# An RMSNorm kernel: two pairs of queued transfers each joined into one

## The chip, the cores and the metric

The kernel runs on one core of a Trainium2 chip. A core has separate engines with their own instruction streams: TensorE (PE in the profile), VectorE (DVE), ScalarE (ACT), GpSimd (POOL) and SyncE (SP), which here only issues transfers. Transfers between the chip's main memory (HBM) and the on-chip memory (SBUF, 128 partitions) are carried out by sixteen DMA engines that all transfers share. The metric is the time of one execution on the device in microseconds. Several executions are timed; one further execution is recorded by the profiler.

## The reference

Every row of 512 values is divided by the root of its mean square and multiplied by gamma:

```python
def setup_inputs():
    batch, seq, dim = 16, 1024, 512
    return {
        "x": np.random.randn(batch, seq, dim).astype(np.float32),
        "gamma": np.ones(dim, dtype=np.float32),
    }

def reference(x, gamma):
    eps = 1e-5
    rms = np.sqrt(np.mean(x ** 2, axis=-1, keepdims=True) + eps)
    return (x / rms * gamma).astype(np.float32)
```

The input is 16,384 rows, 33.55 MB, and the output has the same size.

## The kernel before

The 16,384 rows are cut into four tiles t = 0 to 3 of 128 partitions times 32 rows (`R = 32`); one partition holds 32 rows that lie one after another in HBM, 64 KB. A tile is thus 8.39 MB, and "rows a to b" of a tile means rows a to b - 1 of every partition, so 16 rows are 4.19 MB. Three tiles fit in SBUF: `slots[0..2]`. Tile 3 is loaded into slot 0, so it can be loaded only when tile 0 has been stored from there. Results are written over the data in the slot and stored from there.

Work goes in nine groups (`groups`, L76): tile 0 in rows 0:7, 7:16 and 16:32, every other tile in two halves 0:16 and 16:32. For each group:

- ScalarE squares the rows in pieces of 7, 5, 4 (or 9) rows, and VectorE sums the squares of each row (`square_sums`, L96 and L97). The squares lie in PSUM (`sq_psum`) or SBUF (`sq_sbuf`).
- `inverse_rms`: ScalarE takes the root (L102) and VectorE the reciprocal (L103).
- The last rows of the group (`share`, mostly 7) are multiplied by GpSimd alone, by the row factor and then by gamma (`scale_by_pool`, L109 and L110). The other rows (mostly 9) are multiplied by the row factor on ScalarE, one instruction per row (`scale`, L118), and then by gamma on VectorE in one instruction for all of them (`times_gamma`, L122).

The order is written by hand (`tc.manual_schedule()`); each engine takes its instructions in program order. The loop (L163) handles the scaling of group k and, interleaved with it, the squares and sums of group k + 1: first GpSimd's scaling, then the first two pieces of squares of the next group, then half of ScalarE's row scalings, the third piece of squares, the rest of the row scalings, VectorE's multiplication by gamma, and last the transfers that this group makes possible (`transfers`, L129) and the next group's root and reciprocal. So on ScalarE, the squares of the first half of tile 3 stand ahead of the row scalings of the second half of tile 2.

Loads (`load`, L45) are all issued by SP. Stores (`store`, L49) are issued by SP too, but for three small ones of 4 rows that ScalarE issues: rows 0:4 and 4:8 of tile 0 and rows 0:4 of tile 1. A queue of transfers is worked off in the order of issue; an issue waits on the issuing engine until all that it depends on is done, and what stands behind it in that engine's program waits too. A store waits for VectorE and GpSimd to have finished its rows. A load of tile 3 waits for the completion of the stores that empty its part of slot 0. An instruction that reads loaded rows waits for the whole transfer that brings them.

SP's program is: rows 0:1 and 1:8 of tile 0, gamma in five pieces, rows 8:16 and 16:32 of tile 0, both halves of tile 1, rows 0:23 of tile 2; then, when the group (0, 16) is done, what L133 to L138 list; then the stores of tile 1 rows 4:32, of all of tile 2, and of both halves of tile 3. Rows 23:32 of slot 2 are loaded late because they serve as room for squares of 9 rows until then (L91).

Of the kernel before, what the change touches and what calls it, by code (L numbers as in the profile page):

```python
# [9 lines left out]
def kernel(  # L10
# [33 lines left out]
    def load(t, slot, r0, r1):  # L44
        dma = nc.sync.dma_start(out=slots[slot][:, r0:r1], in_=xv[t][:, r0:r1])  # L45
        before_scale.append((slot, r0, r1, dma))

    def store(t, slot, r0, r1, queue=nc.sync):
        dma = queue.dma_start(out=ov[t][:, r0:r1], in_=slots[slot][:, r0:r1])  # L49
        before_scale.append((slot, r0, r1, dma))  # L50
# [78 lines left out]
    def transfers(t, g):  # L129
        if (t, g) == (0, 0):  # L130
            load(1, 1, 16, 32)
            load(2, 2, 0, 23)
        elif (t, g) == (0, 16):  # L133
            store(0, 0, 8, 16)
            store(0, 0, 16, 32)
            load(2, 2, 23, 32)
            load(3, 0, 0, 16)
            load(3, 0, 16, 32)  # L138
        elif (t, g) == (1, 16):
            store(1, 1, 4, 32)  # L140
        elif (t, g) == (2, 16):
            store(2, 2, 0, 32)
        elif (t, g) == (3, 0):
            store(3, 0, 0, 16)
        elif (t, g) == (3, 16):
            store(3, 0, 16, 32)
# [16 lines left out]
    for k, group in enumerate(groups):  # L163
        t, g, n, pieces, share = group
        mine = n - share
        half = (mine + 1) // 2
        ahead = groups[k + 1 :][:1]
        ss, todo = pieces_of(ahead[0]) if ahead else (None, [])
        scale_by_pool(rstd, t, g, n, share)
        for piece in todo[:2]:  # L170
            square_sums(*piece)
        if (t, g) == (0, 7):
            store(0, 0, 0, 4, nc.scalar)
        scale(rstd, t, g, 0, half)
        for piece in todo[2:]:
            square_sums(*piece)
        scale(rstd, t, g, half, mine)
        if (t, g) == (0, 16):
            store(0, 0, 4, 8, nc.scalar)
        elif (t, g) == (2, 0):  # L180
            store(1, 1, 0, 4, nc.scalar)
        times_gamma(t, g, 0, mine)
        transfers(t, g)
        for nxt in ahead:
            rstd = inverse_rms(ss, nxt[2])
# [30 lines left out]
```

## Time and profile before

| | us |
|---|---|
| median of 3 runs | 161.56 (161.45 to 161.64) |
| the profiled execution | 161.69 |
| its span, first to last instruction | 159.8 |
| DVE busy in the span | 112.0 (70%) |
| ACT busy | 107.8 (67%) |
| POOL busy | 106.4 (67%) |
| moved by DMA in the span | 67.12 MB, mean 420 GB/s |

The span is what the trace covers; 1.9 us of the profiled execution lie around it. The profile divides the span into 40 slices and gives each engine's busy share as a digit; the DMA line is the mean share of the sixteen DMA engines. A DMA queue q1 carries what SP issues, q10 what ScalarE issues. "Us to landing" is the time from the issue of a transfer to its completion, so it contains the time spent behind earlier transfers. The trace also has a record of each DMA packet (one packet per partition and transfer of x or out here, so eight on each of the sixteen engines); where start and end of a transfer on the DMA engines are named, they are read from these records.

### The profile page before, as it was taken

The numbers are of one execution on the slowest core, as the hardware profiler recorded it, in microseconds if no ns is written. First come the engines' busy times: TensorE is split into PE (matmuls) and PEld (weight loads), VectorE is DVE, ScalarE is ACT, GpSimd is POOL, SyncE is SP. The second block draws the span as 40 slices with busy tenths as digits, with TensorE's granted clock in tenths as the row PEclk, the third lists the DMA queues.
The fourth block names the chain that finished last, engine by engine and source line by source line (L and its number), as shares of the span: only waits on it lengthen the run. The fifth ranks groups of instructions, "written<-read, shape, count | busy, mean of one in ns | idle before, by whom it ended". The sixth has DMA issues, their size and how long they took to land.

```text
span 159.8 us, 273 instructions
## 1 busy us (share of the span) xinstructions
PE 2.0 (1%) x2; PEld 0.5 (0%) x2; DVE 112.0 (70%) x39; ACT 107.8 (67%) x108; POOL 106.4 (67%) x24
## 2 busy tenths in 40 slices
PE   0050000000000000000000000000000000000000
PEld 0010000000000000000000000000000000000000
DVE  0019098899798999999999999999999009800000
ACT  3071966975999999999899999989970990000000
POOL 1000960994999599999999999999999990000000
DMA  5999999999999998998999999999996997999995
GB/s 179 431 427 468 443 418 410 377 449 408 455 476 443 443 410 365 423 500 370 434 468 394 470 445 390 501 459 459 459 476 279 525 476 312 394 468 451 394 435 222
DMA packets 2747, 67.12 MB, mean 420 GB/s; under 512 B 313, under 2 KB 314, under 8 KB 442
## 3 DMA queue, kind: packets, MB, share of 16 engines
q1 hardware_dynamic: 2314, 63.97, 93.5%
q10 hardware_dynamic: 432, 3.15, 4.7%
q14 instruction: 1, 0.01, 0.0%
HBM read 33.56 MB, written 33.55 MB: 420 GB/s over the span
## 4 chain that ended last, share of the span: by engine, by line
DVE 59%; ACT 21%; DMA 4%; issue 1%; ACTq 1%; SPq 0%
DVE ss L97 36%; DVE slot L122 23%; ACT slot L118 8%; ACT slot L96 8%; ACT sq_psum L96 5%; DMA slot<-in_x_dram 4%; DVE ss L103 1%; ACT ss L102 0%; ACTq L211 0%; ACT gamma_b L162 0%; SPq L45 0%; ACTq L49 0%; ACTq L96 0%
## 5 line engine op out<-in xcount | busy, mean ns | idle before, releaser
L109 POOL TENSOR_TENSOR slot<-slot,ss 128x3584 f32<-128x3584 f32 (+2 forms) x9 | 46.9, 5213 | 24.2 <-DVE ss L103 24.2
L110 POOL TENSOR_TENSOR slot<-slot,gamma_b 128x3584 f32<-128x3584 f32 (+2 forms) x9 | 59.2, 6582 | 0.7
L97 DVE TENSOR_REDUCE ss<-sq_psum 128x7 f32<-128x3584 f32 (+1 forms) x13 | 42.2, 3245 | 13.7 <-ACT sq_psum L96 13.7
L118 ACT ACTIVATE slot<-slot,ss 128x512 f32<-128x512 f32 x75 | 47.2, 706 | 4.7 <-DVE ss L103 4.7
L122 DVE TENSOR_TENSOR slot<-slot,gamma_psum 128x4608 f32<-128x4608 f32 (+2 forms) x9 | 41.3, 4589 | 8.7 <-ACT slot L118 8.7
L96 ACT ACTIVATE sq_psum<-slot 128x3584 f32<-128x3584 f32 (+1 forms) x13 | 34.5, 2657 | 6.3 <-DMA slot<-in_x_dram 5.7
L97 DVE TENSOR_REDUCE ss<-slot 128x9 f32<-128x4608 f32 x3 | 14.9, 4954 | 4.4 <-ACT slot L96 4.2
L97 DVE TENSOR_REDUCE ss<-sq_sbuf 128x5 f32<-128x2560 f32 x5 | 14.0, 2800 | 0.0
L96 ACT ACTIVATE slot<-slot 128x4608 f32<-128x4608 f32 x3 | 12.1, 4032 | 0.0
L96 ACT ACTIVATE sq_sbuf<-slot 128x2560 f32<-128x2560 f32 x5 | 11.6, 2324 | 0.3 <-DMA slot<-in_x_dram 0.3
L102 ACT ACTIVATE ss<-ss,eps_t 128x16 f32<-128x16 f32 (+2 forms) x9 | 2.7, 304 | 11.7 <-DVE ss L97 11.7
L103 DVE RECIPROCAL ss<-ss 128x16 f32<-128x16 f32 (+2 forms) x9 | 2.1, 235 | 0.4 <-ACT ss L102 0.4
L66 PE MATMUL gamma_psum<-gamma_row,ones_col 1*128 1x512 f32 x2 | 2.0, 1122 | 8.7 <-DMA gamma_row<-in_gamma_dram 8.7
L72 ACT ACT_TABLE_LOAD x1 | 1.3, 1283 | 1.2 <-PEq L200 1.2
L162 ACT COPY gamma_b<-gamma_psum 128x512 f32<-128x512 f32 x1 | 0.6, 564 | 0.0
L66 PEld LDWEIGHTS gamma_psum<-gamma_row,ones_col 1*128 1x128 f32 x2 | 0.5, 305 | 8.6 <-issue 8.6
L64 POOL MEMSET ones_col<- 1x128 f32 x1 | 0.2, 194 | 0.3 <-POOLq L200 0.3
L200 POOL MEMSET const-float32-0.0<- 128x1 f32 x1 | 0.1, 98 | 0.2 <-issue 0.2
L72 ACT ACTIVATE table<-eps_t 128x1 f32<-128x1 f32 x1 | 0.2, 202 | 0.0
L200 POOL MEMSET const-bfloat16-1.0<- 128x1 bf16 x1 | 0.1, 101 | 0.0
L200 POOL MEMSET const-uint8-127<- 128x1 uint8 x1 | 0.1, 101 | 0.0
L200 POOL MEMSET const-float32-1.0<- 128x1 f32 x1 | 0.1, 98 | 0.0
(1 smaller groups left out, 0.1 us busy)
## 6 DMA issues: line engine op xcount, KB each, us to landing
slot<-in_x_dram SPq DMA_DIRECT2D x5, 4096.0 KB, 25.0
out_dram<-slot SPq DMA_DIRECT2D x3, 4096.0 KB, 20.2
out_dram<-slot SPq DMA_DIRECT2D x1, 7168.0 KB
slot<-in_x_dram SPq DMA_DIRECT2D x1, 5888.0 KB
out_dram<-slot ACTq DMA_DIRECT2D x3, 1024.0 KB
slot<-in_x_dram SPq DMA_DIRECT2D x1, 2304.0 KB, 25.7
slot<-in_x_dram SPq DMA_DIRECT2D x1, 2048.0 KB, 10.0
out_dram<-slot SPq DMA_DIRECT2D x1, 2048.0 KB
```

Source lines behind the costliest of these rows:

```text
L66: nc.tensor.matmul(gamma_psum[:, 0], ones_col, gamma_row, start=True, stop=True)
L72: nc.scalar.activation(out=table, in_=eps_t, func=AF.Sqrt)
L96: nc.scalar.activation(out=sq[:, :m], in_=rows, func=AF.Square)
L97: nc.vector.tensor_reduce(out=ss[:, r : r + m, 0], in_=sq[:, :m], axis=mybir.AxisListType.X, op=OP.add)
L102: nc.scalar.activation(out=ss[:, :n, 0], in_=ss[:, :n, 0], func=AF.Sqrt, bias=eps_t, scale=1.0 / D)
L103: nc.vector.reciprocal(out=ss[:, :n, 0], in_=ss[:, :n, 0])
L109: nc.gpsimd.tensor_tensor(out=part, in0=part, in1=by_row, op=OP.mult)
L110: last = nc.gpsimd.tensor_tensor(out=part, in0=part, in1=gamma_b.to_broadcast([P, share, D]), op=OP.mult)
L118: nc.scalar.activation(out=x[:, g + r, :], in_=x[:, g + r, :], func=AF.Copy, scale=rstd[:, r])
L122: scaled = nc.vector.tensor_tensor(out=part, in0=part, in1=gamma_psum.to_broadcast([P, r1 - r0, D]), op=OP.mult)
L162: nc.scalar.copy(out=gamma_b[:, 0], in_=gamma_psum[:, 0])
L200: nc = _bacc.Bacc("TRN2", target_bir_lowering=False, num_devices=1)
```

## The change

When group (0, 16) is done, SP issued two stores of tile 0, rows 8:16 and 16:32, and after the rest of tile 2 two loads of tile 3, rows 0:16 and 16:32. Now it issues one store of rows 8:32 and one load of rows 0:32. Nothing else in the program is changed; the same bytes are moved.

```diff
         elif (t, g) == (0, 16):
-            store(0, 0, 8, 16)
-            store(0, 0, 16, 32)
+            store(0, 0, 8, 32)
             load(2, 2, 23, 32)
-            load(3, 0, 0, 16)
-            load(3, 0, 16, 32)
+            load(3, 0, 0, 32)
         elif (t, g) == (1, 16):
             store(1, 1, 4, 32)
```

SP issues 19 transfers instead of 21, gamma's five among them; the order of instructions on the other engines is as before. What waits for what follows the transfers: the store of rows 8:32 waits for both groups in it, the load of tile 3 for every store that empties slot 0, and every instruction that reads tile 3 for the whole load.

## The prediction

> **What bounds the kernel now.** I read the page first: the three compute engines are each busy about 70% of the span, the DMA line of part 2 stands at 9 almost from end to end, and part 3 puts the two hardware queues together at 98% of sixteen engines.
>
> ```profile
> span 159.8 us, 273 instructions
> DMA  5999999999999998998999999999996997999995
> q1 hardware_dynamic: 2314, 63.97, 93.5%
> q10 hardware_dynamic: 432, 3.15, 4.7%
> ```
>
> So the transfers set the end, whatever the chain of waits says (it ends in a DVE multiplication, because it cannot see behind a store that sits in a queue). Queue q1 is SP's, q10 ScalarE's. The question for any change is then whether the queue ever runs empty. Next I asked for SP's issues in order of time, and for DMA answers over short windows, which give the time from issue to landing of one transfer.
>
> SP's issues around the change; columns: start, length, engine, line (a merged row's length runs to the end of its last issue):
>
> ```profile
> 39.78 16.01 SPq L49 DMA_DIRECT2D out_dram<-slot  x2
> 55.83 0.43 SPq L45 DMA_DIRECT2D slot<-in_x_dram  x1
> 66.45 10.20 SPq L45 DMA_DIRECT2D slot<-in_x_dram  x2
> 111.67 0.34 SPq L49 DMA_DIRECT2D out_dram<-slot  x1
> 125.65 13.94 SPq L49 DMA_DIRECT2D out_dram<-slot  x2
> ```
>
> Store 8:16 of the first tile is issued at 39.78, store 16:32 at 55.45 (39.78 + 16.01 less one issue of 0.34), the rest of tile 2 at 55.83, the halves of tile 3 at 66.45 and 76.33, the store of tile 2 at 111.67, the last store at 139.25. From the short windows, the remainder of tile 2 and the first half of tile 3, with us to landing at the end:
>
> ```profile
> slot<-in_x_dram SPq DMA_DIRECT2D x1, 2304.0 KB, 25.7
> slot<-in_x_dram SPq DMA_DIRECT2D x1, 4096.0 KB, 25.1
> ```
>
> They land at 55.83 + 25.7 = 81.5 and 66.45 + 25.1 = 91.55. Twenty-five microseconds for 4 MB that need ten says that each lies behind other work. The pace of the queue comes from the window 80.6:90.3, which holds just the first half of tile 3 (4.19 MB in 9.7 us, nothing else moving):
>
> ```profile
> q1 hardware_dynamic: 144, 4.19, 100.2%
> ```
>
> That is 2.42 us per MB. Who uses that half is in the timeline (start, length, engine, line, operation):
>
> ```profile
> 91.61 0.31 ACT L102 ACTIVATE ss<-ss,eps_t 128x16 f32<-128x16 f32 x1 [0.35 <-DVE ss L97]
> 91.82 3.14 ACT L96 ACTIVATE sq_psum<-slot 128x3584 f32<-128x3584 f32 x1
> 96.52 3.82 DVE L97 TENSOR_REDUCE ss<-sq_psum 128x7 f32<-128x3584 f32 x1
> 105.18 4.94 DVE L122 TENSOR_TENSOR slot<-slot,gamma_psum 128x4608 f32<-128x4608 f32 x1
> ```
>
> The square at 91.82 reads rows 0:7 of tile 3 and starts 0.3 us after they land: no slack on this load. Behind that square, on the same in-order engine, stand the row scalings of tile 2's second half, and behind those DVE's multiplication (105.18 to 110.12) that its store waits for.
>
> **Part one, the merged store.** It removes one issue (0.34 us of SP) and holds back rows 8:16 (2.1 MB) from 39.78 to 55.45, when rows 16:32 are ready. Cover: the load of tile 2's first 23 rows still runs; by the packet records of the trace it ends at 60.6 to 61.1 (first engine to last), 5.2 us after the issue. An issue into an empty queue needs about 1.0 us to its first packet: the first load is issued at 0.74, and the window to 1.7 holds no packet, that to 1.8 two. So the queue does not run dry, the order of bytes stays, and the two stores together still end at 75.7. With the cover gone the price would be up to 1.0 us. Joining two transfers saves what a boundary costs: by the packet records the 6.3 MB take 14.54 us for twelve packets per engine of 1.21 us (14.5), so at most 0.05 us. Cost: 0.
>
> The Trainium skill, page "DMA: Bandwidth & Descriptors", section "Anatomy of one DMA", gives every transfer about 2.0 us of fixed cost beside its bytes; by it two transfers fewer would take 4 us off. The row above (100.2% of the engines busy while transfers queue behind one another) disagrees for queued transfers.
>
> **Part two, the merged load.** Three things move. (a) Its issue: it now waits for the merged store as a whole (76.26), so at 76.33, where the first half had gone out at 66.45. Cover: the remainder of tile 2 moves until 80.6 to 81.1, 4.3 us against 1.0 needed. Bounds: 0, or 0.3 if the 4.6 us that ScalarE's store of 27.41 took to its first packet (in a loaded queue) held here; I take 0, since SP's own transfers follow each other without a hole. (b) SP's following stores wait behind this issue, at 76.33 as before; the next is due at 83.68: 0. (c) The landing. Rows 0:16 no longer have a completion of their own: the square of 91.82 waits for all 8.4 MB. They start at 80.6 and need 8 x 2.42 = 19.35 us on each engine, so the last engine ends at 100.5, and completion takes 0.4 to 0.7 more: 100.9 to 101.2 undisturbed.
>
> ScalarE's store of tile 1's rows 0:4 (1.05 MB, 2.4 us) is issued at 86.70 and may fall inside. Its packets, windows 86:90.3 and 90.3:102.6:
>
> ```profile
> q1 hardware_dynamic: 48, 1.57, 84.7%
> q10 hardware_dynamic: 144, 1.05, 20.2%
> ```
>
> No q10 packet before 90.3; then all of it between the packets of the second half, one 8 KB packet to one of 32 KB. In all three such stores an engine starts three more SP packets after the issue before q10's first. Bounds: 0 and 2.4 us. With SP packets of 64 KB (2.42 us) three of them reach to about 95, which leaves two to alternate with, so two q10 packets of 0.31: 0.6 us. Landing: 101.7, ends 100.9 and 103.6.
>
> The Trainium skill (same page, section "Queues, rings and completion order") has an engine change between queues only after a packet of some 9 to 17 descriptors; by that this store would wait for the whole load and the landing be 101.0. The one-to-one alternation above speaks against it.
>
> **From the landing to the end.** The square starts 0.08 after landing (8.28 to 8.37 at the first load): 101.78, 9.96 late. The ScalarE chain behind it, taken from the iteration where ScalarE did not wait for DVE (81.61 on): square of 7 rows 3.08, of 5 rows 2.23, five scalings 3.06, square of 4 rows 1.80, four scalings 2.54, together 12.7. DVE's reductions keep up (the third ends at 12.5), so DVE's multiplication starts at 114.5 and ends at 119.45: 9.33 late; 0.6 is won back because DVE had been the later one here. SP issues tile 2's store at 119.5; before, 111.67.
>
> Where was the queue meanwhile? The last store is issued at 139.25 and lands 19.7 later, at 158.95; going back from its last packet (158.6) by 10.2, 9.7 and 19.35 us, tile 2's store had its first packets at 119.35. So it had waited 7.7 us in the queue, and the last store 9.1. After the change the queue is empty from 119.4 to 119.9 (the same bytes went before) and the store's first packet comes at 119.5 + 1.0 = 120.5: a hole of 0.6 to 1.1 us. From there DVE runs without a stop as before (110.12 to 139.19 is 29.07), while the DMA needs 29.0 for the two stores in between: the last store is issued at 148.6, first packet 149.6 instead of 148.35. POOL, 1.3 us ahead of DVE's needs before, restarts with the reciprocal at 119.7 and ends its rows of group (3,0) at 133.7; that store is due at 139.8. So 1.0 to 1.2 us later at the end; I take 1.1.
>
> Sum: 161.69 (the profiled execution; 1.9 of it lies around the span) + 1.1 = 162.8. The median of the runs is 0.13 below that execution: 162.7. As a formula: end moves by landing + first-packet delay - 101.46.
>
> **The rivals.** Full mixing: the ScalarE store falls wholly inside the load, as it did in the second half before. Landing 103.6: + 3.0 to 3.1, 164.6. For it: the row of 90.3:102.6. Against: that mixing began only 3.7 us after the issue, with packets half as long.
>
> Hidden after all (the not-slower side): place, the empty queue at 119.4; it decides at landing + delay = 101.46. If ScalarE's store stays out (100.9) and a store needs between its issue's own 0.34 us and 0.56 us to its first packet, nothing is lost: 161.6 (161.9 with the delay of 1.0). For it: the store had 7.7 us of waiting in the queue to give, against 9.3 of delay, so it is close. Against: 1.0 us in the only row with an empty queue, and the early joining of q10.
>
> The packet rule of the Trainium skill above points this way, and so does its HWDGE first-byte figure of about 0.6 us (same page, section "Latency and other measured facts"): with both the time would be 161.7. No run here shows that figure.
>
> Slow issue: the 3.7 to 4.6 us that ScalarE's stores needed to a first packet are the issue itself and not a wait behind fetched packets. At 119.5 that gives a hole of over 4: 3.7 to 4.6 in place of 1.0 is + 3.8 to 4.7, 165.4 to 166.3. Against: the first load's 1.0 us.
>
> Faster: boundaries between transfers cost more than the rows show, and two fewer pay while the stall stays hidden. By the rows the gain is 2 x 0.05 at most, 161.5; more needs a hole that no window shows. By the fixed cost of the Trainium skill's page "DMA: Bandwidth & Descriptors" it would be 4 us, 157.6.
>
> **How the numbers follow.** My forecast (161.9 to 163.6, landing about 101 to 102.4) 0.62; full mixing 0.14; hidden 0.11; slow issue 0.08; faster 0.05. A change within 0.2% (0.32 us) cannot be told from none here. The range leaves out faster and slow issue and reaches from the hidden case to full mixing: 161.5 to 164.7. Faster 0.05, within 0.11, slower 0.84.
>
> **What would show it.** Right: a single wait of ScalarE's square on the load, some 9 to 10 us long, ending near 101.8; POOL and DVE idle behind it; SP's issue of tile 2's store near 119.5 and a dip of the DMA line right there; none at 61 and 80. Wrong: a landing at 103 or later, a dip at 61 or 80, or a DMA line that stays full at 119 with the end unmoved.

## The result, and the profile after

The changed kernel takes 162.96 us (median of 5 runs, 162.92 to 163.33), the kernel before 161.56 us beside it (161.45 to 161.66). The ratio is 1.0089, with a 95% interval of 1.0076 to 1.0101: slower by 0.9%, 1.4 us. The profiled execution took 162.92 us with a span of 161.1.

The page of the changed kernel, part 1's head, the DMA line and the queues:

```profile
span 161.1 us, 270 instructions
DMA  5999999899999999998999696998979969999996
q1 hardware_dynamic: 2026, 63.97, 92.6%
q10 hardware_dynamic: 432, 3.15, 4.6%
```

The bytes are those of before, 63.97 and 3.15 MB; the sixteen engines need the same time for them, but it is a smaller share of a longer span. A slice is 4 us long and a packet of 64 KB is entered at its start, so the 6s and 7s between the 9s do not all mean idleness. The waits of the changed kernel say more (columns: engine and line, whom it waited for, us in total, times, longest):

```profile
POOL slot L109 <- DVE ss L103: 32.8, 5, 15.0
DVE ss L97 <- ACT sq_psum L96: 22.9, 5, 11.4
ACT sq_psum L96 <- DMA slot<-in_x_dram: 15.9, 2, 10.4
```

Before, ScalarE had one such wait on a load in this line, 5.7 us at the start:

```profile
ACT sq_psum L96 <- DMA slot<-in_x_dram: 5.7, 1, 5.7
```

Now there is a second of 10.4 us. The timeline shows which, and what stands behind it:

```profile
102.17 3.16 ACT L96 ACTIVATE sq_psum<-slot 128x3584 f32<-128x3584 f32 x1 [10.37 <-DMA slot<-in_x_dram]
105.37 3.89 DVE L97 TENSOR_REDUCE ss<-sq_psum 128x7 f32<-128x3584 f32 x1 [8.89 <-ACT sq_psum L96]
114.95 4.96 DVE L122 TENSOR_TENSOR slot<-slot,gamma_psum 128x4608 f32<-128x4608 f32 x1 [0.20 <-ACT slot L118]
```

The square of tile 3's first rows started at 91.82 and starts at 102.17; the multiplication of tile 2's second half started at 105.18 and starts at 114.95. From windows and the timeline, the issue of the load at 76.06 with its time to landing, the issue of tile 2's store, and the two last issues:

```profile
slot<-in_x_dram SPq DMA_DIRECT2D x1, 26.1
119.98 0.34 SPq L49 DMA_DIRECT2D out_dram<-slot  x1
134.19 15.22 SPq L49 DMA_DIRECT2D out_dram<-slot  x2
```

The load is complete at 102.15. The store of tile 2 was issued at 111.67 and is issued at 119.98, and the last one at 149.07 (134.19 + 15.22 - 0.34) in place of 139.25. What that does to the queue is seen in the window 117 to 122, forty slices of 0.125 us in which a packet is entered where it starts; first the kernel before, then the changed one:

```profile
DMA  0999999000000000009999990000000000000099
GB/s 0 918 1376 2294 1376 918 459 0 0 0 0 0 0 0 0 0 0 0 1049 1573 2622 2097 524 524 0 0 0 0 0 0 0 0 0 0 0 0 0 0 1573 2621
```

```profile
DMA  9999000000000000000000000000009900000000
GB/s 2753 1376 1376 1376 0 0 0 0 0 0 0 0 0 0 0 0 0 0 0 0 0 0 0 0 0 0 0 0 0 0 3670 4719 0 0 0 0 0 0 0 0
```

Before, the next round of packets starts some 2.1 us after the last round, which is as long as a packet of the store of tile 1 takes (2.12 us). After, 3.5 to 3.8 us pass. By the packet records the engines are idle for 1.55 us each on average between 116 and 124 (time of the window less the packets' time, over the sixteen engines), and for nothing measurable anywhere else where the change could have opened a hole (55 to 65, 76 to 86, 144 to 152). Before, none of the four windows had idle time. The hole is about as long as the loss of 1.4 us.

### The profile page after: what moved, and what is told of

Read it like the earlier page. It is cut to its first block, busy times and chain, and to the rows that moved or that the text cites. A ratio compares the mean times of both kernels' runs of the same rounds, so it can differ in the third digit from the quotient of the medians.

```text
span 161.1 us, 270 instructions
## 1 busy us (share of the span) xinstructions
PE 2.0 (1%) x2; PEld 0.5 (0%) x2; DVE 112.4 (70%) x39; ACT 107.9 (67%) x108; POOL 106.4 (66%) x24
## 3 DMA queue, kind: packets, MB, share of 16 engines
q1 hardware_dynamic: 2026, 63.97, 92.6%
q10 hardware_dynamic: 432, 3.15, 4.6%
## 4 chain that ended last, share of the span: by engine, by line
DMA 33%; DVE 28%; ACT 27%; issue 3%; ACTq 1%; SPq 0%
DMA slot<-in_x_dram 21%; DVE ss L97 14%; DVE slot L122 14%; DMA out_dram<-slot 13%; ACT slot L118 12%; ACT slot L96 7%; ACT sq_psum L96 6%; ACT sq_sbuf L96 1%; ACT ss L102 0%; ACTq L209 0%; ACT gamma_b L160 0%; SPq L45 0%; ACTq L49 0%; DVE ss L103 0%; SPq L49 0%
```

## The experiments

Eight kernels, each timed against the kernel before in the same session (161.61 us in the first four, 161.66 us in the last four). "Idle" is the mean idle time of the sixteen engines by the packet records, as above.

**One part alone, the store.**

```diff
-            store(0, 0, 8, 16)
-            store(0, 0, 16, 32)
+            store(0, 0, 8, 32)
             load(2, 2, 23, 32)
             load(3, 0, 0, 16)
             load(3, 0, 16, 32)
```

> Only the two stores of tile 0 are joined; the load of tile 3 stays in halves. Theory (the joined store is free, since the load of tile 2 covers it until about 61 and the bytes keep their order): 161.5 to 161.7, no stretch of the DMA line below 9 near 61, the first half of tile 3 landing at 91.3 to 91.9, the square that reads it starting without a wait on the load. Both halves are now issued at about 76.2. Rival (holding 2.1 MB back by 16 us opens a hole at 61, or the later issue of the first half at 76 instead of 66 opens one at 80): slower by 0.3 to 1.0, with the landing late by as much.

Measured 161.71 us, ratio 1.0004 (0.9995 to 1.0013). The first half of tile 3 landed at 91.43 and its square started at 91.66, without a wait on the load. No idle time at 55 to 65 or at 76 to 86, although the first half was now issued some 10 us later than in the kernel before. Holding 2.1 MB back costs nothing, and joining them brings nothing.

**One part alone, the load.**

```diff
-            load(3, 0, 0, 16)
-            load(3, 0, 16, 32)
+            load(3, 0, 0, 32)
```

> Only the two loads of tile 3 are joined; tile 0 is stored in two transfers as before. Theory (the whole loss is the load's): the time of the changed kernel, 162.8 to 163.2; the square waits some 10 us for the load, to about 102.2; the store of tile 2 is issued at about 120 into an empty queue. Rival (the store takes part in the loss): between 161.9 and 162.6.

Measured 163.01 us, ratio 1.008 (1.0067 to 1.0094). The load landed at 102.35, the store of tile 2 was issued at 120.16, and the engines were idle 1.53 us behind 119. The whole loss is the load's.

**A load that lands late, but less so.** With the joined store:

```diff
-            load(3, 0, 0, 32)
+            load(3, 0, 0, 24)
+            load(3, 0, 24, 32)
```

> Joined store as in the change, tile 3 loaded as rows 0:24 and 24:32. Theory (a late landing costs nothing until the queue runs dry, that is up to about 8 us of it): rows 0:24 land at 96 to 97, the square waits 4 to 5 us, the multiplication that tile 2's store waits for ends about 4 us later than before, near 114, and the store still joins a queue that is full to 119: 161.4 to 161.8. Rival (every microsecond of that wait reaches the end): 165 to 166. Rival (each microsecond reaches it in the proportion of the changed kernel, 1.4 for 10): 162.1 to 162.3.

Measured 161.64 us, ratio 1.0002 (0.9993 to 1.001). In its waits:

```profile
ACT sq_psum L96 <- DMA slot<-in_x_dram: 10.7, 2, 5.6
```

Of the 10.7 us, 5.6 are the wait at the start that every version has; the other 5.1 are for rows 0:24, which landed at 96.89. The multiplication before tile 2's store started at 109.67, 4.5 us later than in the kernel before, and the store was issued at 114.69 in place of 111.67 (3.0 us later only, since in the kernel before that store had waited last for GpSimd and not for this multiplication). Nothing of it reached the end. So a wait of 5 us is free and one of 10 us costs 1.4: what counts is a threshold, not a price for each microsecond.

**Nothing joined, the order of the halves swapped.** Against the kernel before:

```diff
-            load(3, 0, 0, 16)
             load(3, 0, 16, 32)
+            load(3, 0, 0, 16)
```

> Stores as before, tile 3 in two loads of 16 rows as before, but rows 16:32 ahead of rows 0:16: nothing is joined, and the rows that are needed first come last. Theory (only the time counts at which rows 0:16 are complete): they land at 103.0 to 103.5, since ScalarE's small store falls wholly into the second transfer; end later by landing + 0.84 - 101.46, less the 0.2 by which the changed kernel's profiled execution ran early from its start: 2.2 to 2.7, 163.8 to 164.3. Rival (the size of the one transfer or of its 64 KB packets is what costs): 161.4 to 161.8.

Measured 164.07 us, ratio 1.0144 (1.013 to 1.0158). Rows 0:16 landed at 103.39, the wait was 11.7 us, tile 2's store was issued at 121.19, and the engines were idle for 2.49 us behind 119; the time rose by 2.46. With two transfers of 4 MB in 32 KB packets the loss is larger than with one of 8 MB, because the rows needed first were complete later. The size of a transfer or of its packets is not what costs.

**Nothing beside the load.** The changed kernel, with ScalarE's store of tile 1's rows 0:4 moved into SP's:

```diff
         elif (t, g) == (1, 16):
-            store(1, 1, 4, 32)
+            store(1, 1, 0, 32)
...
-        elif (t, g) == (2, 0):
-            store(1, 1, 0, 4, nc.scalar)
```

> The changed kernel, with the store of tile 1's rows 0:4 taken from ScalarE and put into SP's store of tile 1 (rows 0:32 in one transfer), so that nothing shares the engines with the load of tile 3. Theory (the end moves by landing + 0.84 - 101.46 and by nothing else): the load lands at 100.6 to 101.0, a square's wait of still about 9 us, the store of tile 2 issued at 118.4 to 118.8, its first packet as the queue runs dry: 161.5 to 161.9. Rival (joining the loads costs its loss by itself, through the wait on ScalarE or the one large transfer): 162.7 to 163.1.

Measured 162.06 us, ratio 1.0018 (1.0006 to 1.003): 0.16 us above the range expected. The load landed at 100.83, the square waited 9.0 us, the store of tile 2 was issued at 118.66, and the engines were idle for 0.12 us. The mechanism is as expected and 1.0 of the 1.4 us is gone, although the wait on ScalarE was shortened by 1.4 us only. Of the remaining 0.4 us the hole explains 0.12. By the packet records another 0.18 are not idle time: the last packet of the load on each engine, started at 97.3 to 97.9, took 2.42 to 2.81 us, 2.60 on average, where the packets of 64 KB ahead of it took 2.42. What slowed them this run does not show, and the last 0.1 is within its spread (161.78 to 162.5).

**The hole at 119 filled.** The changed kernel, with a part of tile 2 in the queue earlier:

```diff
+        elif (t, g) == (2, 0):
+            store(2, 2, 0, 16)
         elif (t, g) == (2, 16):
-            store(2, 2, 0, 32)
+            store(2, 2, 16, 32)
```

> The changed kernel, with tile 2 stored in halves, rows 0:16 as soon as their group is done (about 97.5), so that the queue has 4.2 MB in hand at 119. Theory (two holes in a row, both as long, since VectorE needs 29.07 us from one to the other and the transfers between them 29.0; filling the first leaves the second): no dip at 119, a dip of about 1.3 us at 148 to 150 before the last store, 162.7 to 163.1. Rival (the loss is the hole at 119 alone): 161.5 to 161.8.

Measured 163.03 us, ratio 1.0073 (1.0056 to 1.009). No idle time at 119; but the last store was issued at 149.32, when the one before it had just run out. Window 147 to 151, forty slices of 0.1 us:

```profile
DMA  9999779700000000000000000000000990000000
```

The last packets start by 147.8, of 1.21 us each, and the next start at 150.2. The idle time from 144 to 152 is 1.63 us. The hole had moved, not gone.

**The last store issued earlier in part.** The changed kernel, with the last group's multiplication and store in two parts:

```diff
-        times_gamma(t, g, 0, mine)
+        if (t, g) == (3, 16):
+            times_gamma(t, g, 0, half)
+            store(3, 0, 16, 16 + half)
+            times_gamma(t, g, half, mine)
+        else:
+            times_gamma(t, g, 0, mine)
...
-            store(3, 0, 16, 32)
+            store(3, 0, 23, 32)
```

> The changed kernel, with the last group's multiplication by gamma in two instructions of 7 and 6 rows and its store in two of 7 and 9 rows, the first issued at about 142 instead of 149. Theory (the hole at 119 stands, and from it the transfers run 29.0 us without a stop): first hole as in the changed kernel, none at 149, 162.7 to 163.0. Rival (the loss is the late issue of the last store alone): 161.5 to 161.8.

Measured 163.11 us, ratio 1.0075 (1.0059 to 1.0092). Its last issue is at 145.66 (134.40 + 11.60 - 0.34) and the queue does not run dry there, but the hole at 119 is 1.48 us as before. Slightly above the range expected, by 0.11.

**Both.** The edits of the last two together:

> The changed kernel with both: tile 2 stored in halves and the last group in two parts. Theory (each of the two holes is enough for the whole loss, both must go): no dip at 119 nor at 149 although the square waits 10 us for the load as in the changed kernel, 161.4 to 161.8. Rival (the loss has a cause besides these two): above 162.3. Neither gives a time clearly under the kernel before, since its queue never ran dry there.

Measured 161.66 us, ratio 0.9996 (0.9983 to 1.0009), with no idle time in either window. Its waits and, for 147 to 151, its DMA line:

```profile
ACT sq_psum L96 <- DMA slot<-in_x_dram: 16.4, 2, 10.7
```

```profile
DMA  0099999907000069399969699693699966996969
```

The wait of 10.7 us is there as in the changed kernel, and it costs nothing. Neither edit alone moved the time, and both together took the loss away altogether. It is no faster than the kernel before: that one's queue was never dry, and the bytes are the same.

All together, with the landing of the rows that the square reads:

| kernel | landing | idle at 119 | idle at 149 | time less the kernel before |
|---|---|---|---|---|
| store joined alone | 91.43 | 0 | 0 | +0.10 |
| load in 24 and 8 rows | 96.89 | 0 | 0 | +0.03 |
| nothing beside the load | 100.83 | 0.12 | 0 | +0.40 |
| the change | 102.15 | 1.55 | 0 | +1.40 |
| load joined alone | 102.35 | 1.53 | 0 | +1.40 |
| halves swapped | 103.39 | 2.49 | 0 | +2.46 |
| the change, hole at 119 filled | 102.41 | 0 | 1.63 | +1.37 |
| the change, last store in two | 102.36 | 1.48 | 0 | +1.45 |
| the change, both | 102.62 | 0 | 0 | 0.00 |

## Why the prediction was right

**What bounds the kernel.** Right. In every run the time moved by what the DMA engines stood idle, within 0.3 us; compute waits of 5 and of 10.7 us cost nothing where the queue had work.

**Part one.** Right at a cost of 0: the store alone gave +0.10 us, with an interval that holds zero, and no idle time at 61 or at 80. A fixed cost of about 2 us for each transfer, which the Trainium skill's page "DMA: Bandwidth & Descriptors" gives in "Anatomy of one DMA", is not seen for transfers that stand behind others in the queue: one transfer fewer here changed nothing. The section's figure is a fit to transfers that GpSimd issues; the two joined here are issued by SP.

**Part two, the issue and the landing.** The later issue was covered, as taken. The pace written as 2.42 us per MB is that of 1,048,576 bytes (4.19 million bytes in 9.7 us are 2.31 us per million); the sum counts eight of these and comes out. The landing was 102.15 where 101.7 had been taken between 100.9 and 103.6. The term that was off is the share of ScalarE's small store: "two q10 packets of 0.31: 0.6 us". By the packet records it was four, one ahead of each of the load's last four packets, and on most engines a fifth ahead of the load's completion, 1.2 to 1.55 us. The step that failed is "three of them reach to about 95": only one SP packet started on most engines between the issue at 86.58 and q10's first (fifteen first packets of q10 start at 90.05 to 90.47, the sixteenth at 92.80). The run with nothing beside the load measured the term: 100.83 against 102.15, 1.3 us, though that run's last load packets took up to 0.4 us longer than the others.

By the rule on changing queues in the Trainium skill, page "DMA: Bandwidth & Descriptors", section "Queues, rings and completion order", as the prediction reads it, q10 would have come only behind the whole load, with an estimated landing of 101.0. That reading takes one packet record of the trace as one of the rule's descriptors, which the trace does not say. The trace does not agree with it: between 90 and 101.7 it shows 94 packets of q10 beside 85 of q1, completions included.

```profile
q1 hardware_dynamic: 85, 4.54, 89.6%
q10 hardware_dynamic: 94, 0.77, 15.5%
```

By the packet records the two queues took turns here, mostly one record each.

**From the landing to the end.** The chain behind the square was taken as 17.67 us from its start to the end of the multiplication; it was 17.74 (102.17 to 119.91). The 0.6 us that were to be won back were so: the square is 10.35 late, the multiplication 9.77. The delay from issue to first packet in an empty queue, taken as 1.0 from the first load, was 0.84 (119.98 to 120.82), and 0.83 to 0.85 in the five other runs whose queue ran dry. From there 29.1 us went to the issue of the last store, as forecast, and the transfers in between were just done.

One reading ahead of this was incomplete. In the kernel before, the store of tile 2 waited for DVE's multiplication, done at 110.12, but last for GpSimd, done at 111.65:

```profile
103.85 7.80 POOL L110 TENSOR_TENSOR slot<-slot,gamma_b 128x3584 f32<-128x3584 f32 x1
```

In the changed kernel GpSimd is done at 111.46 and the store waits for DVE alone, so its issue moved by 8.3 us where the multiplication moved by 9.8. The forecast of the new issue did not use that reading.

**The sum.** 162.7 was forecast, 162.96 measured; +1.14 against +1.40 beside the runs of before. The landing was 0.45 later than taken, and the first packet 0.16 earlier: +0.29, which leaves the sum within 0.03 us of the result. Part of that is luck. The prediction's own formula gives 1.24 with its landing of 101.7 and its delay of 1.0, where the sum took 1.1; with the measured 102.15 and 0.84 it gives 1.53. That is the length of the hole (1.55), and 0.13 more than the measured loss: in the profiled execution of the changed kernel the packets ahead of the hole ended some 0.25 us earlier than in the kernel before (119.11 to 119.55 against 119.35 to 119.88), so its end moved by 1.23 only (161.69 to 162.92), while the medians moved by 1.40.

**The rivals.** Full mixing did not come about (102.15, not 103.6), but the kernel with the halves swapped showed it: landing 103.39 and +2.46. The hidden case failed at its two conditions: the landing was above 100.9, and the first packet took 0.84. It is nearly what was seen when nothing stood beside the load (100.83, 0.12 us idle). The slow issue is out: 0.84 us. Nothing was gained by fewer transfers.

## What to carry to other kernels

Where the transfers are the bound, ask of every edit only whether the queue runs empty somewhere; a compute engine may wait long without cost, up to a threshold that can be read off. The issue of the next store may move by the time that the store spends in the queue before its first packet, less the delay into an empty queue: here 119.35 - 111.67 - 0.84 = 6.8 us. ScalarE could wait longer still, because other engines had been later: GpSimd by 1.5 us than DVE, and DVE by 0.6 than ScalarE, which gives an estimated 9 us. The runs that store tile 2 whole agree: a wait of 5.1 us cost nothing, 9.0 left a hole of 0.12, 10.4 one of 1.55. Joining queued transfers saved nothing here, but it delayed the consumer of the first rows until the last had landed. When a delay passes two points at which the queue is equally near to empty, filling one of them gives nothing; both have to be filled.

## What the runs showed that was not expected

What a small store on the other queue waits for before its first packet is not a fixed number of packets. ScalarE's store of tile 1's rows 0:4 was issued at 86.6 to 86.7. Beside packets of 32 KB (the kernel before) q10 began 3.65 us after the issue (86.70 to 90.35), when an engine had started about three more SP packets; beside packets of 48 KB (the load in 24 and 8 rows) it was 4.71 us (86.61 to 91.33) and two; beside packets of 64 KB (the change) 3.47 us (86.58 to 90.05) and one. I had carried over the three packets. A time of about 3.4 us, after which the packet under way is still finished, fits these three (an estimate from the starts), but ScalarE's store of 27.41 needed 4.56 us beside packets of 32 KB. Whether it is a time or an amount of data was not tried; the 0.84 us into an empty queue show that the issue alone does not make it up.

The kernel with nothing beside the load took 0.28 us more than its idle time explains. 0.18 of them are packets that took longer than others of their size, and why they did stays open. Idle time alone therefore does not count all that the engines lose.
